# Two transformer blocks on one core: the first MoE's experts by falling count, four of them with 32 slots, and its fallback branch in mid-stage

## The chip, the cores and the metric

The kernel runs on one core of a Trainium2 chip. Its time is the device time of one execution in microseconds. The profile is of one execution. PE is TensorE's matmuls, PEld its weight loads, DVE is VectorE, ACT ScalarE, POOL GpSimd, SP SyncE, whose only work here is to issue DMAs.

## What is computed

256 tokens of width 1024 pass through two blocks of two layers each. The change lies in `grouped_moe` of the first block, which runs in both of its layers. Every token chooses one of four groups of experts and two of the four experts in it, so there are 512 choices over 16 experts of hidden width 512:

```python
scores = sigmoid(xt @ router_w)
sel = scores + router_b
group_score = top_k(sel.reshape(-1, 4, 4), 2)[0].sum(-1)      # best group per token
idx = top_k(where(in_best_group, sel, -inf), 2)               # two experts per token
combine = scores at idx, divided by their sum
for e in range(16):
    h = silu(xt @ w_gate[e]) * (xt @ w_up[e])
    out = out + combine[:, e:e + 1] * (h @ w_down[e])
x = layer_norm(ALPHA * x + out)
```

The second block begins with a mixer (`even`) that adds a table of relative position biases to its attention scores. All numbers are fp32.

## The kernel before

**Stages.** The stages run one after the other: mixer A, the first MoE of layer 0 (`moe1`, 141 to 387 us of the span, then its layer norm), mixer B, the first MoE of layer 1 (515 to 757 us, then its layer norm), mixer `even`, a dense FFN, mixer `odd`, and a second MoE with 8 wider experts (`moe2`).

**Loads.** All weights come as chunks of 128 x 2048 fp32 (1 MiB) in one fixed list, the `Stream` (L53). SP issues their DMAs in this order into a ring of 18 places: 12 of the pool `raw` and 6 of the pool `hl`. A DMA can be issued when its place is free, that is when the matmuls that read the chunk 18 earlier are done, and when the DMA that had the same one of 8 completion semaphores before it has landed. An expert of the first MoE has six chunks: gate and up, two each (0 to 3), and down (4 and 5). `pipe1` (L1981) lists them expert by expert: four of expert e, then the two of e - 1.

**One stage of `moe1`** (L924). `route1` gives for each token and expert a weight `cb` and a position `pm` among the expert's tokens, and `cnt`, the count of each expert. Before the loop one fallback test is prepared from the largest count. The loop then runs over the experts 0 to 15 in this order. For every fourth expert, `gather` builds one-hot matrices `S` (DVE) for four experts with 64 slots each, 256 columns, and multiplies the tokens with them, in two fp32r parts (`xth`, `xtl`): 32 matmuls `gps`, whose results are copied to `xe` by ACT and DVE. Per expert:

- `gate_up`: `slot_rows` turns the expert's columns of `pm` and `cb` with four transposes (`slps`) and makes the selection `sT` and the scale `gs` on DVE; then `pair` (L299) multiplies 64 slots with gate and then with up: the two column halves of 256 run side by side, one into partitions 0 to 63 of the output and one into 64 to 127. ACT takes Silu and DVE multiplies (`h`).
- `down` of the expert before it (`yps`), then `slot_out`: ACT scales and rounds to fp32r (`sy`), DVE makes the remainder.
- `hidden`: two transposes of `h` (`tr`), copied by ACT.
- `scatter` of the expert before it: eight fp32r matmuls with 64 rows add its slots to the four accumulators `ya` in PSUM, which hold all 256 tokens.

Of layer 1's expert 0 the first half is computed densely ahead of the stage (`part`). A fp32 matmul has two records in the trace, an fp32r one has one.

**The branch.** After the loop `rest1` (L1063) reads the largest count into a register of PE, DVE, ACT and SP, and if it is over 64 all experts are computed densely for the tokens over the limit. It isn't taken here. Its body has thousands of PE instructions, which PE jumps over. At that place SP waits for all outstanding DMAs. Then `ln_banks` (L501) does the layer norm, DVE statistics first, under 24 matmuls `warm` that keep PE busy, then `lnT` (transposes of the normalised pieces) and the first matmuls of the next stage (`begin`).

**The bias table.** In layer 1 `rel_bias` (L1087) loads a table and a one-hot matrix ahead of expert 1, and ahead of experts 6 to 9 does one matmul each (`bps`), a copy (`tb`) and a DMA to DRAM (`bscr`), which `even` reads back in skewed order (`bias`).

**The order of instructions.** The framework orders each engine's instructions by a model of costs, except where an order is written out (`order`, `manual_schedule`); it moves instructions ahead within a stretch without branches. A branch ends such a stretch on the engines that take part.

The second MoE has already what the change brings to the first: experts by falling count, loads whose address is read from a register (`index2`), and small experts with 32 slots, `quad` (L306) with four matmuls side by side.

Of the kernel before, what the change touches and what calls it, by code (L numbers as in the profile page):

```python
# [41 lines left out]
C_N = 687  # L42

# [90 lines left out]
class Banks:  # L134
# [5 lines left out]
    def tile(self, shape, dt, name, tag=None):  # L140
        if self.pool is not None and tag not in self.tags:
            return self.pool.tile(shape, dt, name=name, tag=tag)
        self.n += 1
        return self.k.p_ps.tile(shape, dt, name=name, tag=f"b{self.banks[self.n % len(self.banks)]}")

# [83 lines left out]
class Kern:  # L229
# [271 lines left out]
    def ln_banks(self, pre, src, gb, pp, begin=None, add=None):  # L501
# [25 lines left out]
        self.warm(WARM)  # L527
# [348 lines left out]

    def turned_hidden(self, h, hh, hl, g, u, pg, tag, after=None):
# [45 lines left out]
    def moe1(self, layer, stream, x, xt, fill, began, begin):  # L923
# [5 lines left out]
        with ExitStack() as st:  # L929
# [17 lines left out]
            bigi = self.most(pool, cnt)  # L947
# [4 lines left out]
            with ExitStack() as st2:  # L952
# [5 lines left out]
                def gather(es):  # L958
                    n = 4
                    S = w2.tile([128, 2, 4, CAP1], F32R, name="S", tag="S", bufs=1)  # L960
                    for t in range(2):
                        nc.vector.tensor_tensor(S[:, t, :n], self.iota[:, None, :CAP1].to_broadcast([128, n, CAP1]),
                                                pm[:, t, es[0]:es[0] + n, None].to_broadcast([128, n, CAP1]), op=OP.is_equal)
                    xs = w2.tile([128, 8, 4, CAP1], F32, name="xe", tag="xe", bufs=1)
                    for i, e in enumerate(es):
                        xe[e] = xs[:, :, i]
                    for k in range(8):
                        ps = pp.tile([128, 4, CAP1], F32, name="gps", tag="mm")
# [7 lines left out]

                def gate_up(e):
                    if e % 4 == 0:
                        gather(range(e, e + 4))
                    slots[e] = self.slot_rows(w2, pp, pm, cb, e, self.c[:, C_CIDX:C_CIDX + 1])  # L980
                    x64 = xe.pop(e)
                    ps = pg.tile([128, 2, 256], F32, name="gu", tag="gu")
# [11 lines left out]
                def hidden(e, h):  # L994
                    ps = pp.tile([128, 2, 2, CAP1], F32, name="tr", tag="mm")
# [9 lines left out]
                def down(e):  # L1005
                    ps = pp.tile([128, 512], F32, name="yps", tag="mm")
                    fs = (1,) if part(e) else (0, 1)
                    for f in fs:
                        w = stream.get(1024, ahead=1 if e == E1 - 1 and f else None)
                        self.pair(ps, [(hs[e][:, k, f], w[k][0][:, 0:512], w[k][0][:, 512:]) for k in range(2)], f == fs[0], f == 1)  # L1010
# [3 lines left out]
                def scatter(e):  # L1014
                    for t in range(2):
                        for c in range(2):
                            if e == 0:
                                self.mm(ya[t][c], self.ident, pre[:, t, half(c, 512)], True, False)
                        for i in range(2):
                            for c in range(2):  # L1020
                                r = half(c, 64)
                                self.mm(ya[t][c], slots[e][0][r, half(t)], ys[e][i][r, :], False, e == E1 - 1 and i == 1)
                    del slots[e], ys[e]

                for e in range(E1 + 1):
                    if layer == 1 and e in (1, 6, 7, 8, 9):
                        self.rel_bias(w2, max(e - 5, 0), pp)
                    h = gate_up(e) if e < E1 else None
                    if e == E1:
                        begin.allow()  # L1030
                        stream.prepare(3)
                    if e > 0:
                        down(e - 1)
                    if e < E1:
                        hidden(e, h)
                    if e == E1:
                        begin.load()
                        gb = self.load_ln(2 * layer + 1)
                    if e > 0:
                        scatter(e - 1)  # L1040
            self.rest1(layer, bank, x, cb, pm, bigi, part)
            xt = self.ln_banks(pre, bank, gb, Banks(self, (0, 1)), begin)
# [15 lines left out]
    def left(self, pool, pm, cb, cap, n):  # L1058

        w = pool.tile([128, 2, n], F32, name="left")  # L1060
        self.nc.vector.tensor_scalar(w, pm, float(cap), None, op0=OP.is_ge)
        self.nc.vector.tensor_tensor(w, w, cb, op=OP.mult)
        return w  # L1063

    def rest1(self, layer, bank, x, cb, pm, bigi, part):

        nc, tc = self.nc, self.tc
        rv = nc.values_load(bigi[0:1, 0:1], engines=BRANCH, min_val=0, max_val=T)
        with tc.If(rv > CAP1):
            with ExitStack() as st:  # L1070
                p1 = st.enter_context(tc.tile_pool(name=f"rest{layer}", bufs=1))
                pg, py = Banks(self, (0, 1)), Banks(self, (2, 3))
                room = st.enter_context(tc.tile_pool(name=f"rr{layer}", bufs=2))
                wt = self.left(p1, pm, cb, CAP1, E1)
                xt = self.turned(x, pg, "rg", True)
                for e in range(E1):
                    fs = (1,) if part(e) else (0, 1)
                    w = Stream(self, self.chunks1(layer, e, [j for f in fs for j in (2 * f, 2 * f + 1, 4 + f)]), ahead=0, room=room)
                    self.dense1(w, xt, wt, e, fs, bank, p1, pg, py)

    def chunks1(self, layer, e, which, whole=True):

        i = (layer * E1 + e) * 6
        return [(self.a["w_moe1"][i + j], 2, whole) for j in which]


    def rel_bias(self, pool, h, pp):  # L1087


        nc, a = self.nc, self.a  # L1090
        if h == 0:
            self.bscr = self.p_d.tile([4, 23, 512], F32, name="bscr")
            self.relt = pool.tile([32, 4], F32, name="relt", bufs=1)
            nc.sync.dma_start(self.relt, a["relt"])
            self.oh = pool.tile([32, 512], F32, name="oh", bufs=1)
            nc.sync.dma_start(self.oh, a["oh"])
            return
        h -= 1
        rb = pool.tile([32, 128], F32, name="relb", bufs=1)
        nc.vector.tensor_copy(rb, self.relt[:, h:h + 1].to_broadcast([32, 128]))  # L1100
        ps = pp.tile([128, 512], F32, name="bps", tag="mm")
        nc.tensor.matmul(ps, rb, self.oh, start=True, stop=True)
        tb = pool.tile([128, 512], F32, name="tb", bufs=1)
        nc.scalar.activation(tb, ps, AF.Copy)
        nc.scalar.dma_start(self.bscr[h], tb[0:23])
# [427 lines left out]
    def route2(self, pool, w2, pp, ps):  # L1533
# [28 lines left out]
        self.ranked = (idxi, {})  # L1562
# [33 lines left out]
    def index2(self, r):  # L1596

        idx, regs = self.ranked
        if r not in regs:
            regs[r] = self.nc.values_load(idx[0:1, r:r + 1], engines=[ET.SP], min_val=1, max_val=E2 - 1)  # L1600
# [32 lines left out]
    def chunks2(self, jobs):  # L1633
# [3 lines left out]
        def chunk(r, j):  # L1637
# [4 lines left out]
            return (lambda: w[bass.ds(self.index2(r), 1), j].rearrange("o p f -> (o p) f")), 2, r >= HEAVY  # L1642
# [9 lines left out]
    def moe2(self, stream, x, xt, began, ln, out):  # L1652
# [5 lines left out]
        with ExitStack() as st:  # L1658
# [76 lines left out]
            def down(r, s, h):  # L1735
# [21 lines left out]
                def collect(q, y):  # L1757
                    if "small" not in ys:
                        ys["small"] = w2.tile([128, 1024], F32, name="yq", bufs=1)
# [207 lines left out]
    def run(self, out):  # L1967
# [13 lines left out]
        def pipe1(layer, part):  # L1981

            c = []
            for e in range(E1 + 1):
                if e < E1:
                    c += self.chunks1(layer, e, (2, 3) if part and e == 0 else (0, 2, 1, 3))
# [238 lines left out]
```

## Time and profile before

| | us |
|---|---|
| three runs | 1957.87, 1952.04, 1956.91 |
| median | 1956.91 |
| the profiled execution | 1956.97 |
| its span, first to last instruction | 1955.2 |
| PE busy in the span | 1822.1 (93%) |
| DVE, ACT, POOL busy | 892.0, 735.9, 297.8 |
| DMA, mean over the span | 301 GB/s |
| mean granted clock of PE | 0.976 of 2.4 GHz |

Busy time counts overlapping records once, and the ends of matmuls are modelled: consecutive groups overlap by 0.07 to 0.2 us in the rows, so the time of a group is best read from its start to the next one's start. A DMA share of 1.0 means that all 16 DMA engines are busy. Idle time stands in square brackets with what ended it.

### The profile page before, as it was taken

The numbers are of one execution on the slowest core, as the hardware profiler recorded it, in microseconds if no ns is written. First come the engines' busy times: TensorE is split into PE (matmuls) and PEld (weight loads), VectorE is DVE, ScalarE is ACT, GpSimd is POOL, SyncE is SP. The second block draws the span as 40 slices with busy tenths as digits, with TensorE's granted clock in tenths as the row PEclk, the third lists the DMA queues.
The fourth block names the chain that finished last, engine by engine and source line by source line (L and its number), as shares of the span: only waits on it lengthen the run. The fifth ranks groups of instructions, "written<-read, shape, count | busy, mean of one in ns | idle before, by whom it ended". The sixth has DMA issues, their size and how long they took to land. (4 is left out here: it accounts for less than half of the span.)

```text
span 1955.2 us, 36295 instructions
## 1 busy us (share of the span) xinstructions
PE 1822.1 (93%) x15228; PEld 1424.6 (73%) x15228; DVE 892.0 (46%) x1631; ACT 735.9 (38%) x1205; POOL 297.8 (15%) x129
## 2 busy tenths in 40 slices
PE   9999999899999998998999988899998889999896
PEld 8885555488655555897999867787777778987753
DVE  5661121267411113467101476655556568866412
ACT  5531111054211111652444364344445456655311
POOL 0310000002000000523888323200000000000000
PEclk9999999999999999999999999899999999999898
DMA  9659999855598894744553240489999999899995
GB/s 381 249 193 409 409 419 419 326 198 191 192 414 347 340 419 168 288 169 159 181 187 130 88 177 23 172 323 391 388 416 418 418 419 415 343 391 419 419 415 231
DMA packets 86031, 589.29 MB, mean 301 GB/s; under 512 B 9782, under 2 KB 11510, under 8 KB 16340
## 3 DMA queue, kind: packets, MB, share of 16 engines
q1 hardware_dynamic: 83042, 580.67, 74.6%
q10 hardware_dynamic: 2802, 6.06, 0.9%
q8 instruction: 126, 2.06, 0.4%
q14 instruction: 61, 0.50, 0.1%
HBM read 585.45 MB, written 1.24 MB: 300 GB/s over the span
## 5 line engine op out<-in xcount | busy, mean ns | idle before, releaser
L103 ACT ACTIVATE whl<-raw 128x1024 fp32r<-128x1024 f32 x426 | 433.1, 1054 | 220.4 <-issue 98.4
L105 DVE TENSOR_TENSOR whl<-raw,whl 128x1024 fp32r<-128x1024 f32 x315 | 375.2, 1228 | 128.1 <-ACT whl L103 125.8
L105 POOL TENSOR_TENSOR whl<-raw,whl 128x1024 fp32r<-128x1024 f32 x111 | 274.3, 2489 | 898.5 <-ACT whl L103 845.2
L287 PE MATMUL sgu<-whl,xe 128*128 128x256 f32 x2064 | 261.2, 287 | 27.2 <-DVE sh L1705 21.5
L287 PEld LDWEIGHTS sgu<-whl,xe 128*128 128x128 f32 x2064 | 252.7, 193 | 36.4 <-DVE sh L1705 26.5
L287 PE MATMUL gu<-raw,xe 128*64 128x256 f32 x1408 | 172.4, 382 | 0.0
L287 PEld LDWEIGHTS gu<-raw,xe 128*64 128x64 f32 x1408 | 102.0, 137 | 53.7 <-issue 5.3
L287 PE MATMUL fgu<-xh,whl 128*128 128x256 f32 x640 | 116.7, 283 | 0.0
L287 PE MATMUL zps<-xh,whl 128*128 128x256 f32 x576 | 111.5, 291 | 2.6 <-ACT xh L276 1.8
L990 ACT ACTIVATE h<-gu 128x256 f32<-128x256 f32 x31 | 11.9, 383 | 253.6 <-PE gu L287 253.6
L1948 POOL TENSOR_TENSOR pre<-pre,lngb 128x512 f32<-128x512 f32 x2 | 2.5, 1259 | 672.5 <-ACT pre L1947 672.5
L287 PEld LDWEIGHTS fgu<-xh,whl 128*128 128x128 f32 x640 | 100.3, 192 | 0.4
L991 DVE TENSOR_TENSOR h<-h,gu 128x256 f32<-128x256 f32 x31 | 13.1, 422 | 184.8 <-ACT h L990 184.8
L287 PEld LDWEIGHTS zps<-xh,whl 128*128 128x128 f32 x576 | 92.8, 195 | 3.9 <-ACT xh L276 2.0
L287 PE MATMUL fgu<-xl,whl 128*128 128x256 f32 x320 | 90.4, 283 | 0.0
L287 PE MATMUL yps<-raw,hT 128*64 128x512 f32 x352 | 89.5, 595 | 0.0
L287 PE MATMUL zps<-xl,whl 128*128 128x256 f32 x288 | 82.7, 287 | 0.8 <-DVE xl L277 0.8
L287 PE MATMUL sy<-whl,shh 128*128 128x512 f32 x264 | 82.7, 394 | 0.0
L1688 ACT ACTIVATE sh<-sgu 128x256 f32<-128x256 f32 x43 | 16.5, 383 | 159.1 <-PE sgu L287 159.1
L317 DVE SCALAR_TENSOR_TENSOR sy<-yps,gs,sy 128x512 fp32r<-128x512 f32 x32 | 24.0, 751 | 113.7 <-ACT sy L316 113.7
L287 PE MATMUL gu<-whl,xe 128*64 128x256 f32 x608 | 75.5, 383 | 0.0
L1380 DVE TENSOR_TENSOR fh<-fh,fgu 128x512 f32<-128x512 f32 x10 | 6.9, 689 | 139.7 <-PE fgu L287 139.7
(490 smaller groups left out, 3180.5 us busy)
## 6 DMA issues: line engine op xcount, KB each, us to landing
raw<-in_w_moe_dram SPq DMA_DIRECT2D x399, 1024.0 KB, 11.9
whl<-in_w_moe_dram SPq DMA_DIRECT2D x57, 1024.0 KB, 11.0
raw<-in_w_dense_dram SPq DMA_DIRECT2D x53, 1024.0 KB, 7.0
raw<-in_w_ffn_dram SPq DMA_DIRECT2D x33, 1024.0 KB, 6.0
lngb<-in_lnp_dram ACTq DMA_DIRECT2D x8, 512.0 KB, 4.5
lngb<-in_lnp_dram SPq DMA_DIRECT2D x8, 512.0 KB, 5.0
xraw<-in_xT_dram SPq DMA_DIRECT2D x4, 256.0 KB
raw<-in_w_dense_dram SPq DMA_DIRECT2D x2, 512.0 KB, 4.7
```

Of the source, the lines that this page charges most:

```text
L103: nc.scalar.activation(hi, r, AF.Copy)
L105: on.tensor_tensor(lo, r, hi, op=OP.subtract)
L287: self.nc.tensor.matmul(out, lhsT, rhs, start=start, stop=stop, skip_group_check=True)
L317: self.nc.vector.scalar_tensor_tensor(yl, ps, gate, yh, op0=OP.mult, op1=OP.subtract)
L990: nc.scalar.activation(h, ps[:, 0, :], AF.Silu)
L991: nc.vector.tensor_tensor(h, h, ps[:, 1, :], op=OP.mult)
L1380: nc.vector.tensor_tensor(h, h, g[1], op=OP.mult)
L1688: nc.scalar.activation(h, ps[:, 0, :], AF.Silu)
L1948: nc.gpsimd.tensor_tensor(v, v, gb[0][:, half(c, 512)], op=OP.mult)
```

## The change

- `ranks1`, new, sorts experts 3 to 15 by falling count after the first gather (DVE), gives the sorted `pms` and `cbs`, an index per rank and a limit per expert: 64 slots, and 32 for the four of rank 9 to 12.
- The loop runs in `ORDER`: experts 0 to 2 as they are, then ranks, the four light ones (12 to 15) in places 4, 5, 7 and 8. Their loads are register-addressed.
- A gather serves 3, 6 (two with 64 slots, four with 32), 4 and 3 experts.
- A light expert uses `quad`, has its output collected in `yq`, and the four share one `slot_rows` and one `scatter` with 128 slots.
- The register load for the branch stands after place 11 and the branch after place 13, with the largest excess over the limits; the fallback's tiles lie in those of the stage.
- `rel_bias` moves to the end of layer 0, after its loop, with all four heads and one DMA; its loads are on ACT's queue behind the branch. `ln_banks` of layer 0 has 6 `warm` instead of 24.

```diff
+FIXED = 3
+LIGHT = range(E1 - 4, E1)
+ORDER = [0, 1, 2, 3, 12, 13, 4, 14, 15, 5, 6, 7, 8, 9, 10, 11]
+GROUPS = [[0, 1, 2], [3, 4, 12, 13, 14, 15], [5, 6, 7, 8], [9, 10, 11]]
...
+    def ranks1(self, layer, pool, tmp, pm, cb, cnt):
+        n = E1 - FIXED
+        sq, sh = [128, n, n], [128, 2, n, n]
+        nc.vector.scalar_tensor_tensor(key, cnt[:, FIXED:], 16.0, self.iota[:, 0:n], op0=OP.mult, op1=OP.subtract)
+        nc.vector.tensor_tensor(gt, key[:, None, :].to_broadcast(sq), key[:, :, None].to_broadcast(sq), op=OP.is_gt)
+        nc.vector.tensor_reduce(rank, gt, axis=AX.X, op=OP.add)
...
+        self.ranked = (idxi, {}, layer * E1 + FIXED, layer * E1 + E1 - 1)
+        for name, src in (("pms", pm), ("cbs", cb)):
+            nc.vector.tensor_tensor(v, perm[:, None].to_broadcast(sh), src[:, :, None, FIXED:].to_broadcast(sh), op=OP.mult)
+            nc.vector.tensor_reduce(o[:, :, FIXED:], v, axis=AX.X, op=OP.add)
...
                 def gate_up(e):
-                    if e % 4 == 0:
-                        gather(range(e, e + 4))
-                    slots[e] = self.slot_rows(w2, pp, pm, cb, e, self.c[:, C_CIDX:C_CIDX + 1])
+                    if e in LIGHT:
+                        ps = pg.tile([128, 2, 128], F32, name="lgu", tag="gu")
+                        for i in range(2):
+                            w = enumerate(zip(stream.get(256), stream.get(256)))
+                            self.quad(ps[:, i, :], [(x64[:, k], *(v[0][:, half(j)] for v in (g, u) for j in range(2))) for k, (g, u) in w])
+                        nc.scalar.activation(v[up], ps[lo], AF.Silu)
+                        nc.vector.tensor_tensor(v[up], v[up], ps[up], op=OP.mult)
+                        return h
+                    rows(e)
...
                 def down(e):
+                    if e in LIGHT:
+                        ps = pp.tile([128, 256], F32, name="lps", tag="mm")
+                        for i in range(2):
+                            w = stream.get(1024)
+                            self.quad(ps, [(hs[e][:, i, half(k, 32)], *(w[k][0][:, half(j, 256)] for j in range(4))) for k in range(2)], i == 0, i == 1)
+                        for j in range(4):
+                            nc.scalar.activation(ys["light"][half(e - LIGHT[0], 32), half(j, 256)], ps[half(j, 32)], AF.Copy)
+                        return
...
                 def scatter(e):
+                    if e in LIGHT:
+                        if e != LIGHT[-1]:
+                            return
+                        rows(LIGHT)
+                        y = [self.slot_out([v[:, c] for v in room], ys["light"][:, half(c, 512)], slots[LIGHT][1]) for c in range(2)]
+                        for i in range(2):
+                            for t in range(2):
+                                for c in range(2):
+                                    self.mm(ya[t][c], slots[LIGHT][0][:, half(t)], y[c][i], False, False)
+                        return
...
-                for e in range(E1 + 1):
-                    if layer == 1 and e in (1, 6, 7, 8, 9):
-                        self.rel_bias(w2, max(e - 5, 0), pp)
+                for i, e in enumerate([*ORDER, None]):
+                    if i == 0:
+                        gather(groups[e], pm)
+                        pms, cbs, cap, bigi = self.ranks1(layer, pool, w2, pm, cb, cnt)
+                    elif e in groups:
+                        gather(groups[e], pms)
...
+                    if i == E1 - 5:
+                        rv = nc.values_load(bigi[0:1, 0:1], engines=BRANCH, min_val=0, max_val=T)
+                    if i == E1 - 3:
+                        self.rest1(layer, w2, bank, x, cb, pm, cap, rv, part)
+                        if layer == 0:
+                            rel = self.rel_load(w2)
+                if layer == 0:
+                    self.rel_bias(*rel, w2, pg)
-            self.rest1(layer, bank, x, cb, pm, bigi, part)
-            xt = self.ln_banks(pre, bank, gb, Banks(self, (0, 1)), begin)
+            xt = self.ln_banks(pre, bank, gb, Banks(self, (0, 1)), begin, warm=WARM if layer else 6)
...
+    def rel_load(self, pool):
+        nc.scalar.dma_start(relt, a["relt"])
+        nc.scalar.dma_start(oh, a["oh"])
+        nc.vector.tensor_copy(rb, relt[:, :, None].to_broadcast([32, 4, 128]))
+        return rb, oh
+    def rel_bias(self, rb, oh, pool, pp):
+        for h in range(4):
+            ps = pp.tile([128, 512], F32, name="bps")
+            nc.tensor.matmul(ps, rb[:, h], oh, start=True, stop=True)
+            nc.scalar.activation(tb[0:23, h], ps[0:23], AF.Copy)
+        nc.scalar.dma_start(self.bscr.rearrange("h p f -> p h f"), tb[0:23])
...
+        return [(lambda j=j: w[bass.ds(self.index(e - FIXED), 1), j].rearrange("o p f -> (o p) f"), 2, whole) for j in which]
```

## Rows read from the trace of the kernel before

**Rows 1.** Windows of both stages: from:to, length, busy per engine, clock, DMA share, GB/s.

```profile
141.20:386.73 245.53, 238.73 (x1667) 131.73 (x1665) 42.59 (x109) 29.53 (x66) 0.00 (x0) 1.00 0.97 395
...
515.30:757.35 242.05, 236.06 (x1614) 128.84 (x1612) 45.16 (x112) 31.40 (x70) 0.00 (x0) 1.00 0.88 354
```

**Rows 2.** Windows inside the first stage and near its end.

```profile
220.00:235.00 15.00, 15.00 (x112) 8.28 (x110) 2.73 (x7) 1.34 (x3) 0.00 (x0) 1.00 1.01 420
...
359.00:361.00 2.00, 2.00 (x20) 1.19 (x18) 0.00 (x0) 0.25 (x1) 0.00 (x0) 1.00 0.04 16
```

**Rows 3.** Timeline of SP's issues: start, us to the last issue, what, count.

```profile
332.52 12.19 SPq L76 DMA_DIRECT2D raw<-in_w_moe_dram  x6
...
503.42 13.64 SPq L76 DMA_DIRECT2D whl<-in_w_moe_dram  x5
```

**Rows 4.** Timeline of PE around ordinary experts.

```profile
278.91 0.43 PE L844 MATMUL slps<-consts,pm 128*128 128x128 f32 x2
...
291.84 0.43 PE L844 MATMUL slps<-consts,pm 128*128 128x128 f32 x2
...
385.22 1.51 PE L287 MATMUL ya<-sy,sT 64*128 64x512 f32 x8 [0.79 <-ACT sy L316]
```

**Rows 5.** Timelines of PE and DVE in the second MoE, experts with 32 slots.

```profile
1495.18 1.96 PE L287 MATMUL sgu<-raw,xq 128*32 128x128 f32 x64
1496.95 1.05 PE L287 MATMUL sy<-raw,lhT 128*32 128x256 f32 x16
...
1887.21 0.33 PE L844 MATMUL slps<-consts,slsp 128*128 128x128 f32 x1
...
1889.42 3.67 PE L287 MATMUL sgu<-raw,xl 128*64 128x256 f32 x32
...
1891.27 1.41 DVE L317 SCALAR_TENSOR_TENSOR sy<-yq,gs,sy 128x512 fp32r<-128x512 f32 x2 [0.79 <-ACT sy L316]
...
1900.59 2.12 PE L287 MATMUL fy<-sy,sT 128*128 128x512 f32 x8
```

**Rows 6.** A group of PE instructions by form; the first stage's window, `gps` alone.

```profile
L287 PE MATMUL begin<-raw,xf 128*128 128x256 f32 x192 | 44.5, 385 | 0.0
...
141.20:386.73 245.53, 20.67 (x128) 16.50 (x128) 6.80 (x16) 6.14 (x16) 1.00 0.97 395
```

**Rows 7.** The branch's line on SP and PE (ns; first and last start); PE's stops.

```profile
L1069 SPq EVENT_SEMAPHORE  x16: 17/17/17, 360.4 to 745.6; - x16
L1069 SPq COMPARE_BRANCH  x2: 45/48/50, 348.7 to 728.7; - x2
...
L1069 PEldq COMPARE_BRANCH  x2: 3549/4891/6233, 386.7 to 757.2; - x2
...
386.73:392.97 6.24, 0.00 (x1) 0.00 (x0) 6.03 (x20) 0.00 (x0) 0.00 (x0) 0.69 0.78 315
757.35:760.84 3.49, 0.01 (x2) 0.00 (x0) 1.10 (x2) 0.00 (x0) 0.00 (x0) 1.00 0.04 9
```

**Rows 8.** Timelines of DVE, PE and ACT at the ends of stages.

```profile
391.00 1.67 DVE L515 SCALAR_TENSOR_TENSOR pre<-pre,lnrs,lngb 128x256 f32<-128x256 f32 x4
...
393.11 4.12 PE L287 MATMUL warm<-bfconst 128*128 128x256 bf16 x24 [6.38 <-PEq L1069]
397.06 0.38 PE L535 MATMUL lnT<-consts,pre 128*128 128x128 f32 x2
...
767.50 0.38 ACT L536 ACTIVATE xf<-lnT 128x256 f32<-128x256 f32 x1 [11.72 <-DVE lnv L405]
...
1107.18 2.79 PE L287 MATMUL warm<-bfconst 128*128 128x256 bf16 x24
```

**Rows 9.** Bias matmuls (PE), the count (DVE), and SP's waits in layer 1's stage.

```profile
511.46 0.16 DVE L811 COPY cnt<-posps 128x16 f32<-128x16 f32 x1
...
614.97 1.12 PE L1102 MATMUL bps<-oh,relb 32*128 32x512 f32 x2
...
SPq L76 <- DMA bscr<-tb: 57.6, 4, 18.4
```

More of the change, by code (lines that the diff above doesn't have):

```diff
@@ L499, in out_proj, with ln_banks @@
         return pre, xt
-    def ln_banks(self, pre, src, gb, pp, begin=None, add=None):
+    def ln_banks(self, pre, src, gb, pp, begin=None, add=None, warm=WARM):
         nc = self.nc
@@ L526, in ln_banks @@
         xf = self.p_raw.tile([128, 8, 256], F32, name="xf", tag="raw")
-        self.warm(WARM)
+        self.warm(warm)
         for t in range(2):
@@ L994, in hidden @@
                 def hidden(e, h):
+                    if e in LIGHT:
+                        ps = pp.tile([128, 2, 64], F32, name="tr", tag="mm")
+                        for j in range(2):
+                            nc.tensor.transpose(ps[:, j], h[up, half(j)], self.ident[up, up])
+                        hs[e] = w2.tile([128, 2, 64], F32, name="lhT", tag="hT", bufs=1)
+                        nc.scalar.activation(hs[e], ps, AF.Copy)
+                        return
                     ps = pp.tile([128, 2, 2, CAP1], F32, name="tr", tag="mm")
@@ L1067, in rest1 @@
         nc, tc = self.nc, self.tc
[L1068 to L1087, printed above, removed]
-        nc, a = self.nc, self.a
[L1091 to L1105, printed above, removed]
+        with tc.If(rv > 0):
+            p1 = Rooms(w2, {"left": "left", "rhh": "yq", "rh": "S"})
+            pg, py = Banks(self, (0, 1)), Banks(self, (2, 3))
+            room = InTurn(self.p_c, ("lng", "lnb"))
+            wt = self.left(p1, pm, cb, cap, E1)
+            xt = self.turned(x, pg, "rg", True)
+            for e in range(E1):
+                fs = (1,) if part(e) else (0, 1)
+                w = Stream(self, self.chunks1(layer, e, [j for f in fs for j in (2 * f, 2 * f + 1, 4 + f)]), ahead=0, room=room)
+                self.dense1(w, xt, wt, e, fs, bank, p1, pg, py)
@@ new lines, in chunks1 @@
+    def chunks1(self, layer, e, which, whole=True, ranked=False):
+        w = self.a["w_moe1"]
+        if not ranked or e < FIXED:
+            return [(w[layer * E1 + e, j], 2, whole) for j in which]
+        return [(lambda j=j: w[bass.ds(self.index(e - FIXED), 1), j].rearrange("o p f -> (o p) f"), 2, whole) for j in which]
+    def rel_load(self, pool):
+        nc, a = self.nc, self.a
+        relt = pool.tile([32, 4], F32, name="relt", bufs=1)
+        nc.scalar.dma_start(relt, a["relt"])
+        oh = pool.tile([32, 512], F32, name="oh", tag="S", bufs=1)
+        nc.scalar.dma_start(oh, a["oh"])
+        rb = pool.tile([32, 4, 128], F32, name="relb", tag="yq", bufs=1)
+        nc.vector.tensor_copy(rb, relt[:, :, None].to_broadcast([32, 4, 128]))
+        return rb, oh
@@ L1983, in pipe1 @@
             c = []
-            for e in range(E1 + 1):
-                if e < E1:
-                    c += self.chunks1(layer, e, (2, 3) if part and e == 0 else (0, 2, 1, 3))
-                if e > 0:
-                    c += self.chunks1(layer, e - 1, (5,) if part and e == 1 else (4, 5))
+            for e, last in zip([*ORDER, None], [None, *ORDER]):
+                if e is not None:
+                    c += self.chunks1(layer, e, (2, 3) if part and e == 0 else (0, 1, 2, 3) if e in LIGHT else (0, 2, 1, 3), ranked=True)
+                if last is not None:
+                    c += self.chunks1(layer, last, (5,) if part and last == 0 else (4, 5), ranked=True)
             return c
@@ L2202, in expert @@
         return [g[0], u[0], g[1], u[1], _chunk(d[:256], 0, D), _chunk(d[256:], 0, D)]
-    a["w_moe1"] = np.stack([c for l in range(2) for e in range(E1) for c in expert(l, e)])
+    a["w_moe1"] = np.stack([np.stack(expert(l, e)) for l in range(2) for e in range(E1)])
     a["w_ffn"] = np.stack(_gate_up(f["ffn_w_gate_2"][0], f["ffn_w_up_2"][0]) + _downs(f["ffn_w_down_2"][0]))
```

119 lines of the change are left out of this document (88 added, 31 removed).

## The prediction

> **What bounds the kernel now.** I read the stretches of the two expert stages first, then TensorE's instructions in order of time, then the load queue, and last the branch. In both stages TensorE is busy for 97 and 98% of the stretch at a granted clock of 1.00, which is 2.4 GHz [rows 1]. The weight loads are close behind: in the middle of the first stage the DMA share is 1.01 at 420 GB/s [rows 2], so a chunk of 1 MiB takes 2.5 us and the six of an expert 15.0 us. An ordinary expert costs TensorE 12.93 us from one `slps` to the next [rows 4], and each group of four a gather of 32 `gps` matmuls. So two streams of nearly the same pace run beside each other, and what matters is how far loads run ahead. The last load of the first stage was issued before 345 us [rows 3], nothing moved at 359 to 361 us [rows 2], and the last matmuls that read a chunk ended at 384.4 us, where the wait before the last `ya` begins [rows 4]: loads were done some 25 us before their last use. The path to the end of a stage is therefore TensorE's, and it can be cut by some 20 to 25 us before loads set the pace. In the second stage loads had slack (share 0.88, [rows 1]).
>
> **Light experts, per layer.** Four experts leave the ordinary path: 4 x 12.93 = 51.7 us. In their place each does gate and up with 32 columns: second-MoE rows of the same form show 1.96 us for 64 records of `sgu` and 1.05 us for 16 of `sy` per slice of 256 [rows 5], two slices per expert: 6.0 us, and its transposes some 0.4 (as now, inside the 12.93): 4 x 6.4 = 25.6 less the overlaps of some 0.1 us at each change of group, 23.5. Once per layer come four transposes with a copy ahead of each (1887.21 to 1889.42: 2.2 us) and eight scatter matmuls with 128 slots (2.1 us) [rows 5]. Sum 27.8, so -23.9. The scatter also waits for selection, scale and split, which in the second MoE were hidden behind other matmuls; with nothing to hide them it costs 3.2 (from the last transpose, 1889.4, to the end of the second split, 1892.7 [rows 5]); I take 1.6. Some experts of the later half wait 0.79 us for `sy` before `ya` [rows 4], early ones don't. If all twelve do, +5, if none, -6; I take +2, because the branch cuts the stretch over which instructions are ordered together.
>
> **Gathers.** The groups become 3, 6, 4 and 3 experts: 192, 256, 256 and 192 columns. Now four gathers of 256 columns take 20.7 us, 5.2 each and 0.16 per matmul [rows 6]. No row has fp32r under 256 columns. From below it costs three quarters (-1.3 us per gather). From above it loses its single pass and costs three quarters of what plain fp32 with 256 columns does: 192 records, two per matmul, in 44.5 us [rows 6], 0.46 us each, so 0.35 against 0.16, 32 x 0.19 = +6 per gather. Four such gathers: -5 to +24. I take the nearest row, the same operands at 256 columns: 0.
>
> **Branch in the middle, per layer.** Now TensorE stands still behind the branch: 6.24 us in the first layer, DMA share 0.78, and 3.49 us in the second, share 0.04 [rows 7].  In the middle of the stage the share is 1.01, so by the line through these two points the stop is 7.1 us. Behind it TensorE starts at a lower clock: 24 `warm` matmuls took 4.12 us after the stop and 2.79 where nothing stopped [rows 8], so I add 1.5. Sum 8.6; bounds 3.5, and 17 if it stands as long as SP does at its branches (11.7 and 16.9 us from its compare to its first event after it [rows 7]). Queued behind the branch on PE are the next expert's `gu` matmuls, which ACT, DVE and the loads' slots wait for. SP's stop also makes a hole in the loads: the DMA share of 0.04 at 359 to 361 us is that hole [rows 2]. It lies now after the last expert's chunks and will lie 13 chunks earlier; about 4 us of lead, no time while lead is left.
>
> The Trainium skill (Runtime: NRT & Kernel Launch, Instruction fetch mechanics) says that a taken branch whose target isn't among the pages held forces a fetch by DMA before execution goes on. By that rule the fetch stands in line with loads, which the two stops at shares 0.04 and 0.78 bear out; the sum by the rule alone would reach for the upper end, 8 us more per layer, and by the row of an idle DMA 4 us less.
>
> **End of the stages.** In layer 0 `warm` began after the stop and `lnT` at 397.06 us, while DVE had its first normalised piece at 391.5 [rows 8]. After the change PE does four bias matmuls of the form `bps` there (1.12 us for one [rows 9], some 4.2 in all; their copies are on an idle ACT) and 6 instead of 24 `warm`: `lnT` at about 392.0, -5.0. The path behind it is PE's own. In layer 1 ACT issued the DMAs of the next block until 767.5, after PE's release at 760.8, and only then copied `lnT` [rows 8]; without the stop of 3.5 us all of it is that much earlier: -3.5.
>
> **Bias table.** In layer 1 four `bps` go from TensorE's path: -4.2. Four waits of SP for `bscr` (57.6 us in total [rows 9]) go too; they cost no time now, but loads. In layer 0 the two small loads on ACT's queue and the copy of `relt` come after the branch; if DVE waits for the landing, up to 5 us in front of the next `h`; the later `gu` (7 us) hides it, 0.
>
> **Ranks and loads.** DVE adds some 25 small operations per layer at its idle start; the second stage's five loads at 503.42 to 517 us [rows 3] are partly of ranked experts and must now wait for the ranks, which can't come before `cnt` at 511.5 [rows 9] plus seven operations and SP's register load, about 515. Five loads are 12.5 us of lead. With the light experts in the first half TensorE gains 24 us on the loads up to the ninth expert, about what the lead is at the end, so it may then wait for loads: 0 to 4 us in layer 0, 0 to 10 in layer 1; I take 1 and 4. Register-addressed loads themselves exist in the second MoE and cost SP some 0.2 us against 2.5 per chunk: 0.
>
> **Sum.** Layer 0: -23.9 + 1.6 + 2 + 8.6 + 1 - 5.0 = -15.7. Layer 1: -23.9 + 1.6 + 2 + 8.6 + 4 - 4.2 - 3.5 = -15.4. Together -31.1. The profiled execution took 1956.97 us (span 1955.2 and 1.8 around it), the median of three is 1956.91, so no correction: 1926 us. Its own range, from the bounds of branch (-5 to +8 per layer) and bubbles, mostly independent, 1914 to 1940.
>
> **Rivals.**
> *Narrow gathers are slow.* All terms as above and +24 for four gathers of 192 columns at the plain fp32 pace: 1950 us. For it: moe2's gathers of 128 columns use plain fp32. Against it: the 256-column rows are not bound by columns alone (weight loads of 128 columns stand beside them).
> *Loads set the pace (slower).* If the lead is used up early, the light experts give nothing, since every chunk is still loaded. Then the hole of SP at the branch (4 us) and the wait for the ranks (5) cost in full in both layers and so does the chain at the branch (8.6), against -5.0, -3.5 and -4.2: 2 x 17.6 - 12.7 = +22, 1979 us. It decides from the point where the landing is less than some 2 us ahead of its use before the ninth expert; the 25 us at the end of the first stage speak against it, the share of 1.01 for it.
> *The fallback runs.* The change lowers four limits to 32. If an expert among the last four had more than 32 tokens, all 16 are computed densely, 96 more chunks x 2.5 = 240 us in that layer. Counted from the reference's inputs, the lightest four of experts 3 to 15 have 27, 24, 19, 15 tokens in layer 0 and 24, 22, 22, 16 in layer 1, and no expert over 53: not taken.
> *More than forecast.* Branch at 3.5 without a clock loss, gathers at three quarters, no waits for loads or bubbles: -31 - 10 - 5 - 5 - 4 = -55, 1902 us.
>
> **Chances.** Forecast 0.52, narrow gathers slow 0.26, loads set the pace 0.10, more than forecast 0.11, fallback 0.01. A measurement of this kernel tells 0.3% (5.9 us) from no change. All of the forecast and of the larger gain is faster, of the slow gathers two thirds (1950 lies at the edge): faster 0.82; same 0.11 (a third of the slow gathers, and a little of the load case); slower 0.07. Eight in ten: 1905 to 1953.
>
> **What would show it.** Right: the light experts' `gu` take 3.9 us and the group from its first `gu` to the next ordinary expert some 7 us less each; one PE stop in mid-stage of about 7 us and none before `warm`; `lnT` about 5 us after the last `ya` of layer 0; share about 1.0 through 600 to 665 us. Wrong: `gps` of 192 columns with 0.3 us of pitch or more; PE waiting for `raw` behind the light experts; a mid-stage stop over 12 us; SP standing at the ranks for over 10 us; SP or DVE waiting for `relt` in layer 0.

## The result, and the profile after

The changed kernel takes 1933.04 us (median of four runs, 1931.05 to 1937.26) against 1954.47 (four runs): ratio 0.9892, 95% interval 0.9874 to 0.9911, or -21.4 us. Forecast were 1926 and a range of 1905 to 1953. The profiled execution took 1931.05 us, span 1929.3, which is 25.9 below the span of before. Of these, 4.6 lie ahead of the change, in code that both kernels share. One line of the windows each, the first 20 us of before and of after (columns as in [rows 1]):

```profile
0.00:20.00 20.00, 15.62 (x84) 13.19 (x85) 10.03 (x14) 10.20 (x15) 0.19 (x4) 0.83 0.87 331
```
```profile
0.00:20.00 20.00, 16.87 (x118) 14.64 (x119) 10.33 (x15) 11.69 (x16) 0.19 (x4) 1.00 0.90 340
```

The execution of before that was profiled began at a granted clock of 0.83, the one of after at 1.00. The later kernels, alike there, reach the matmuls `posps` ahead of the first stage at 135.0 to 138.2 us (before 140.5, after 135.9). Without that start, -21.3 is left, close to the -21.4 of the medians.

The two stages of the changed kernel, which answer to [rows 1], and what PE waited for in each:

```profile
139.60:373.90 234.30, 214.13 (x1935) 122.26 (x1934) 39.86 (x106) 35.87 (x84) 0.00 (x0) 0.99 0.97 396
503.90:732.40 228.50, 205.66 (x1880) 120.34 (x1880) 41.94 (x116) 31.77 (x78) 0.00 (x0) 0.96 0.94 387
```
```profile
PE ya L314 <- ACT sy L343: 6.6, 8, 1.9
PE slps L871 <- PEq L1191: 6.5, 1, 6.5
PE tr L1080 <- DVE h L1061: 2.0, 2, 1.0
PE slps L871 <- ACT yq L1104: 1.7, 1, 1.7
PE gps L314 <- ACT yq L1104: 1.6, 1, 1.6
...
PE ya L314 <- ACT sy L343: 8.2, 10, 1.9
PE slps L871 <- PEq L1191: 6.5, 1, 6.5
PE gps L314 <- DVE xe L1043: 2.0, 1, 2.0
```

(Columns: who waited for what, us in total, times, longest. PEq and ACTq are the sequencers of PE and ACT, here at the branch.) Counted from the first `gps` to the last `ya`, the first stage went from 242.5 to 234.3 us and the second from 237.7 to 228.5. PE, busy for 97% before, now stands still for 20 us of the first and 23 us of the second. Most of that is 6.5 at the branch, 7.1 in the chains of the light experts, 4.7 and 6.3 ahead of the ordinary experts' `ya` (6.3 and 5.5 before), and 2.0 at the first gather of layer 1. It waits nowhere for a chunk.

The light experts in layer 0, PE's timeline (start, us, instruction, idle before):

```profile
228.15 3.70 PE L314 MATMUL lgu<-raw,xe 128*32 128x128 f32 x128
232.82 0.34 PE L1080 MATMUL tr<-consts,h 64*128 64x64 f32 x2 [0.98 <-DVE h L1061]
...
243.66 0.33 PE L1080 MATMUL tr<-consts,h 64*128 64x64 f32 x2 [0.98 <-DVE h L1061]
243.92 1.93 PE L314 MATMUL lps<-whl,lhT 128*32 128x256 f32 x32
247.50 0.50 PE L314 MATMUL gps<-S,xth 128*128 128x256 f32 x2 [1.65 <-ACT yq L1104]
...
264.71 0.33 PE L871 MATMUL slps<-consts,slsp 128*128 128x128 f32 x1 [1.66 <-ACT yq L1104]
...
269.03 2.28 PE L314 MATMUL ya<-sy,sT 128*128 128x512 f32 x8 [1.86 <-ACT sy L343]
```

3.70 and 1.93 us are what [rows 5] foretold (3.9 and 2.1); the five idle times add up to 7.1. The mid-stage stop in layer 0, and the end of that stage:

```profile
328.72 1.52 PE L314 MATMUL ya<-sy,sT 64*128 64x512 f32 x8 [0.42 <-ACT sy L343]
...
336.78 0.66 PE L871 MATMUL slps<-consts,pms 128*128 128x128 f32 x2 [6.53 <-PEq L1191]
...
373.81 0.83 PE L314 MATMUL warm<-bfconst 128*128 128x256 bf16 x6
378.51 1.91 PE L562 MATMUL lnT<-consts,pre 128*128 128x128 f32 x6 [3.87 <-DVE pre L542]
...
381.49 8.00 PE L314 MATMUL begin<-raw,xf 128*128 128x256 f32 x30
```

`lnT` begins 4.6 us after the last `ya`, when DVE has its first piece; in [rows 8] it was 10.3.

### The profile page after: what moved, and what is told of

It reads as the page before. It is cut to its first block, busy times and chain, and to the rows that moved or that the text cites. A ratio compares the mean times of both kernels' runs of the same rounds, so it can differ in the third digit from the quotient of the medians.

```text
span 1929.3 us, 37804 instructions
## 1 busy us (share of the span) xinstructions
PE 1772.0 (92%) x15778; PEld 1410.5 (73%) x15778; DVE 893.7 (46%) x1655; ACT 744.7 (39%) x1233; POOL 297.3 (15%) x129
## 5 line engine op out<-in xcount | busy, mean ns | idle before, releaser
L314 PE MATMUL gu<-raw,xe 128*64 128x256 f32 x960 | 115.2, 390 | 0.0
L314 PEld LDWEIGHTS gu<-raw,xe 128*64 128x64 f32 x960 | 70.8, 141 | 38.4 <-issue 6.5
L1815 DVE TENSOR_TENSOR sh<-sh,sgu 128x256 f32<-128x256 f32 x43 | 18.1, 421 | 113.3 <-ACT sh L1814 113.0
L314 PE MATMUL yps<-raw,hT 128*64 128x512 f32 x288 | 69.3, 597 | 0.0
L314 PE MATMUL gu<-whl,xe 128*64 128x256 f32 x544 | 66.1, 383 | 0.0
```

The lines of the kernel that those rows point to most:

```text
L314: self.nc.tensor.matmul(out, lhsT, rhs, start=start, stop=stop, skip_group_check=True)
L1815: nc.vector.tensor_tensor(h, h, ps[:, 1, :], op=OP.mult)
```

## Experiments

Each kernel is the changed one with the edit shown. Differences to it are the difference of the two ratios to before times 1955 us; with the intervals of both, they are known to some 5 us. All kernels ran on a chip beside the kernel before.

**all64**: no light experts.

```diff
-FIXED = 3
-LIGHT = range(E1 - 4, E1)
+FIXED = 4
+LIGHT = range(E1, E1)
+ORDER = [*range(E1)]
+GROUPS = [[0, 1, 2, 3], [4, 5, 6, 7], [8, 9, 10, 11], [12, 13, 14, 15]]
```

> The changed kernel without light experts: all sixteen keep 64 slots and run in the order 0 to 15 after sorting from the fourth on; four gathers of 256 columns; branch in mid-stage, bias table and 6 warm as in the changed kernel. My theory: the light experts are the one real gain in the stages, 51.7 us of ordinary work against 23.8 (records), 3.2 (scatter), 7.1 (waits of PE for h, yq and sy), and 1.2 less for the narrow gathers, so 18.8 per layer. Without them 37 us slower than the changed kernel, about 1970, which is some 0.8% slower than before. Rival (loads set the pace of the stages, so that PE's saving is partly hidden): under 20 us slower than the changed kernel, below 1953, and PE waiting for raw in the changed kernel's stages instead.

1961.49 us, ratio 1.003 (1.0019 to 1.0041): 27 slower than the changed kernel, and slower than before. So without the light experts the other parts together cost 6 us; which of them cost and which gain, this run does not tell. Of the 37 expected, 10 are missing in the medians, but not in the profiles: from `posps` to the last `ya` the two stages take 17.6 and 14.4 us longer. In layer 0 the stop of all64 was 2.8 shorter, and in layer 1 the changed kernel lost 3.7 at its gather (below); with these it is 20.4 and 18.1 per layer, against 18.8. The profiled run of all64 was the slowest of eight and that of the changed kernel the fastest of four, so part of this is chance. The rival is out: PE waits for no chunk in either kernel.

**end_branch, no_branch, warm24**: the branch behind the stage again; no branch; 24 `warm` in layer 0.

```diff
 # end_branch, in the loop and behind it
-                        self.rest1(layer, w2, bank, x, cb, pm, cap, rv, part)
+            self.rest1(layer, None, bank, x, cb, pm, cap, rv, part)   # tiles in pools of its own, as before
 # no_branch
-                        rv = nc.values_load(...)
-                        self.rest1(layer, w2, bank, x, cb, pm, cap, rv, part)
 # warm24
-            xt = self.ln_banks(..., warm=WARM if layer else 6)
+            xt = self.ln_banks(..., warm=WARM)
```

> The changed kernel with its fallback branch back behind the stage (register loads stay in mid-stage). My theory: the mid-stage stop is a pure loss on PE, 6.5 and the slow clock behind it 1.4 in layer 0, 6.5 and 2.8 in layer 1; at the end the stop lies beside the layer norm's statistics, which hold lnT for 4.6 us anyway, so it costs only what it is longer plus the warm matmuls behind it: about +2 in layer 0 (6 warm) and +3 in layer 1 (24 warm). Together -12 against the changed kernel: about 1921, ratio to before 0.983. Rival (the move was neutral: what the mid-stage stop costs, the end gives back, as the terms 8.6 against -5.0 and -3.5 of the forecast nearly have it): -5 or less, 1928 to 1935.

> The changed kernel without its fallback branch and register load (leaves out the fallback, which these inputs never take). My theory: both stops and the slow clock behind them go and nothing else takes their place, since PE nowhere waits for a load in the changed kernel's stages: -7.9 in layer 0 and -9.3 in layer 1, about 1916, ratio 0.980. Rival (loads catch up: 17 us less of PE leave the chunks late): -8 or less, 1925, with PE waiting for raw in the last four experts.

> The changed kernel with 24 instead of 6 warm matmuls in layer 0's norm. My theory: after 6 of them PE is idle for 3.9 us, the granted clock falls and the first 30 begin records take 8.0 us instead of some 6.6; 24 take 2.8 us, which lies inside the 4.6 us of the statistics, so nothing is added and begin gets its 1.4 us back: -1.4, 1931.6; lnT at the same distance of 4.6 us from the last ya. Rival (the few warm matmuls of the change are what brings lnT forward): lnT 1 to 3 us later and the time +1 to +3.

end_branch: 1922.42, ratio 0.9832 (0.9815 to 0.9848), -12. no_branch: 1914.49, 0.9799 (0.9785 to 0.9813), -18. warm24: 1930.54, 0.9876 (0.986 to 0.9892), -3 and inside the error, but its trace has the 28 `begin` in 6.21 us, 0.22 each against 0.27 above, with `lnT` at the same 4.6 us. end_branch and no_branch came out as the theory had it, in time: the change made the branch dearer by moving it. At the end the stop lies beside statistics that hold `lnT` for 4.6 us anyway (with the stop there `lnT` came 8.3 and 11.3 us after the last `ya`); in mid-stage nothing lies beside it. By layers end_branch's profile, 8.7 us shorter, fits less well. Its stages are 4.0 and 9.2 us shorter (7.9 and 9.3 expected), and the stretches from the last `ya` to the second half of `begin` are 2.2 and 3.9 longer; in layer 0 the clock fell behind the light experts' waits instead (last section). The time of warm24 can't tell its theory from the rival; its trace bears the theory out. In the 18 us of no_branch, loads did not become late: PE waits for no chunk.

**tiny_body**: what the stop is made of.

```diff
-            for e in range(E1):
+            for e in range(0):        # in rest1
```

> The changed kernel with a fallback body of 16 transposes on PE instead of thousands of instructions (leaves out the dense experts of the fallback, which these inputs never take); the test, its register load and its place in mid-stage stay. My theory: the stop is the way over the body, instructions that must be fetched before PE can go on, so with a short body PE stops under 1 us in both layers and the clock does not fall: -7.4 and -8.8, about 1917, ratio 0.981. Rival (the stop belongs to the taken branch itself, or to the busy DMA engines: any jump under load costs it): 6 us in both layers as now, no difference, 1933.

1916.63, ratio 0.9801 (0.9785 to 0.9817), -18: nearly all that no_branch gained. The branch's line on PE, in the changed kernel and with the short body (ns: shortest, median, longest of two):

```profile
L1191 PEldq COMPARE_BRANCH  x2: 6177/6282/6386, 330.2 to 689.2; - x2
```
```profile
L1191 PEldq COMPARE_BRANCH  x2: 228/282/337, 323.5 to 676.8; - x2
```

The taken branch took 0.3 us where it jumps a little way and 6 where it jumps over the fallback. The Trainium skill (Runtime: NRT & Kernel Launch, Instruction fetch mechanics) says that a taken branch to instructions not held must fetch them by DMA before going on; the traces agree. The DMA queues in the changed kernel's stop (330.2 to 336.4 us: packets, MB, share) hold instruction packets, in the short one's (323.4 to 323.8) none:

```profile
q1 hardware_dynamic: 342, 2.54, 99.3%
q8 instruction: 1, 0.02, 1.0%
q14 instruction: 2, 0.02, 0.6%
```
```profile
q1 hardware_dynamic: 23, 0.16, 99.2%
```

By itself this is no proof, since such packets also pass where nothing stops (two in 310.0 to 316.2 us). But in the second stop of the kernel before (757.2 to 760.7 us) they are all that moved:

```profile
q8 instruction: 1, 0.02, 2.1%
q14 instruction: 2, 0.02, 1.8%
```

The edit empties the bodies of the other engines too: ACT's first event comes 0.1 us after its branch, where it took 6.3 and 2.5 in the changed kernel. So the 18 us need not be PE's stop alone; hint, below, parts the two.

**chain, act_gather**: the light experts' waits, and layer 1's first gather.

```diff
 # chain
+                            if j % 2: nc.vector.tensor_copy(dst, ps[half(j, 32)])     # yq: every other copy on DVE
+                        with tc.issue_after(self.last.ins):                           # tr of a light h behind the last down matmul
+                    if i > 1 and ORDER[i - 2] == LIGHT[-1]:
+                        scatter(LIGHT[-1], True)                                      # one expert later, sT and gs in places of their own
 # act_gather
-                        if k % 2:
+                        if k % 2 and not on_act:                                      # on_act: first gather of layer 1
```

> The changed kernel with the light experts' waits loosened: yq's copies shared by ACT and DVE, the common scatter one expert later (under the gate and up of the next), and the transposes of a light h behind the down matmuls of the expert before. My theory: the waits of 0.98 (twice), 1.65, 1.66 and 1.86 us of PE in each stage are chains with nothing beside them; two halve and three go: about -5.4 per layer, 1922, ratio 0.984. Rival (they only move: the next ordinary expert's ya and h then wait in their place): -2 per layer or less, 1929 or more.

> The changed kernel with all eight copies of the first gather on ACT in layer 1. My theory: the DVE operations of the ranking lie ahead of the copies there, PE waits 2.03 us for one of them and then runs 20 gps at a lower clock (4.58 us instead of 2.9): -4 in layer 1, 1929, PE without a wait in that gather. Rival (ACT's copies are then what gps wait for, or the clock was low for another reason): 0 to +2, 1933 to 1935.

chain: 1918.82, ratio 0.9811 (0.9797 to 0.9825), -16, more than the 11 expected; in its profile the stop was 3.4 us in both layers instead of 6.3, which is 5.8 of it and not what the edit aimed at: its branch met DMA engines that were partly idle (last section). PE's waits in layer 0 became

```profile
PE slps L871 <- PEq L1199: 3.6, 1, 3.6
PE ya L314 <- ACT sy L343: 3.3, 6, 0.8
PE slps L871 <- ACT hT L1094: 0.9, 1, 0.9
PE gps L314 <- ACT lhT L1084: 0.5, 1, 0.5
```

so of the 7.1 us 1.4 are left (the last two lines), and they did not move to the ordinary experts. act_gather: 1932.28, 0.9877 (0.9857 to 0.9898), -3, which can't be told from nothing. Its trace has no wait in that gather, but 1.0 us of waits for chunks in layer 1; in both layers the clock then fell at the light experts' waits (their eight `ya` took 3.78 us instead of 2.28).

**bias1**: the bias table back in layer 1.

```diff
+                    if layer == 1 and i in (1, 6, 7, 8, 9):
+                        self.rel_bias(w2, max(i - 5, 0), pp)      # and rel_bias as before
```

> The changed kernel with the bias table built in layer 1 as before (five pieces ahead of experts 1 and 6 to 9 of the order, loads on SP's queue, four DMAs), none of it in layer 0. My theory: a swap of equal work: layer 0 wins some 3.4 us (the four matmuls of 1.1 us there partly fill waits for sy), layer 1 loses 4.2 and SP waits for bscr; no difference that can be told, 1930 to 1936. Rival (the move is worth its own gain, since layer 1's SP waits of 57.6 us delay loads of a stage that now has no slack): 4 us or more slower, 1937, with PE waiting for raw in layer 1.

1942.14, ratio 0.9928 (0.9913 to 0.9942), +7. My expectation of no difference failed; the rival is nearer. Layer 1's stage, from `posps` on, is 10.2 us longer in its profile, and PE waits there for a chunk as it did not before:

```profile
PE lps L314 <- DMA whl<-in_w_moe_dram: 1.9, 1, 1.9
```

The matmuls themselves are 4.5 of it. Part of the rest is the clock: as an estimate, from PE's busy time in windows of 1 us times what the granted clock there lacks of 1.00, bias1 lost 10.3 us in this stage and the changed kernel 7.1. In layer 0, where bias1 has four matmuls fewer, its stage is not 3.4 us shorter, as expected, but 1.3 longer, with 6.3 us lost to the clock against 1.5, most of it ahead of the branch, where both kernels do the same work. So the +7 can't be put down to the bias table alone.

**hint**: the fetch begun early.

```diff
+                    if i == E1 - 3:                                # behind gate_up, ahead of down
+                        with tc.issue_after(self.last.ins):
+                            tc.mark_branch_hint_location(f"rest{layer}", "LikelyTaken", engines=[ET.PE])
-        with tc.If(rv > 0):
+        with tc.If(rv > 0, label=f"rest{layer}"):
```

> The changed kernel with one instruction more on PE per layer: a branch prefetch hint between the gate-and-up and the down matmuls ahead of the branch, some 6 us before it. Body and place of the branch are unchanged. My theory: the stop is the fetch of the instructions behind the body, which begins only at the branch (3.4 to 3.9 us where the DMA engines are idle in its first 3 us, 6.0 to 6.5 where they are busy); begun 6 us ahead it is over in time: stop under 1 us, no clock loss, time as with the short body, 1917, ratio 0.980. Rival (the hint comes to nothing, or its fetch waits behind the weights and ends no earlier than the branch needs it): stop of 3 us or more, 1925 to 1933.

1926.42, ratio 0.9853 (0.9835 to 0.9871), -8: the mechanism holds, the sum does not. The time lies in the rival's range, but not for the rival's reason: PE's branch takes under half a microsecond with the body unchanged, at a DMA share of 1.02 in the 3 us from its start in layer 0:

```profile
L1194 ACTq COMPARE_BRANCH  x2: 50/52/54, 330.8 to 685.9; - x2
...
L1194 PEldq COMPARE_BRANCH  x2: 439/464/488, 331.9 to 686.9; - x2
...
L1194 ACTq EVENT_SEMAPHORE  x2: 17/17/17, 336.2 to 688.6; - x2
```

but ACT also jumps over its body, and its first event behind the branch came 5.4 us later in layer 0 and 2.7 in layer 1. PE then waits for ACT, 1.6 us in layer 1 and in layer 0

```profile
336.27 0.69 PE L871 MATMUL slps<-consts,pms 128*128 128x128 f32 x2 [4.30 <-ACTq L1194]
```

**best1, best2, best3**: the parts together. best1 is end_branch, chain and act_gather with 10 `warm` in layer 1; best2 is hint, chain, act_gather and warm24; best3 adds to best2

```diff
+                        for on, last in ((ET.PE, self.last), (ET.Activation, self.silu)):   # hint on both
-        nc.scalar.dma_start(gup, a["gup"])
+        nc.gpsimd.dma_start(gup, a["gup"])                 # strict, and bias of heads 0 and 1, likewise
```

> Branch behind the stage, loosened light experts and the first gather's copies on ACT together, with 10 instead of 24 warm matmuls in layer 1's norm. My theory: they lie on different stretches of PE's path and add: -11 (branch), -11, -4, and -2 for the fewer warm matmuls behind the stop: about 1905, ratio 0.975. Rival (the loads become the bound once PE has gained 25 us: PE waits for raw in the last experts, and the gains don't add): 1912 or more.

> The changed kernel with the prefetch hint, the loosened light experts, the first gather's copies on ACT in layer 1, and 24 warm matmuls in layer 0's norm. My theory: -16 (hint), -11 (light experts, without the shorter stop that its run had by chance), -2, -2: 1902, ratio 0.974, less some 3 us of waits for raw as they showed in layer 1 with the branch behind the stage: 1905. Rival (loads now set the pace of both stages): PE waits over 8 us for raw and whl, 1910 or more.

> The kernel before this one (prefetch hint on PE, loosened light experts, first gather's copies on ACT in layer 1, 24 warm matmuls in both norms) with two things more: the prefetch hint also on ACT, and the six DMAs of the next mixer's first tables on POOL's queue instead of ACT's at the end of layer 1. My theory: with PE's own fetch hidden, PE waited 1.3 us in each layer for ACT, whose fetch is now hidden too: -2; and ACT's issues, 10 us in a row, stood ahead of its copies of lnT, which made PE wait 5.6 us: -5. Together 1906, ratio 0.975, still some 3.5 us of waits for raw and whl in layer 1. Rival (what waits passes on: the copies come earlier, but begin then waits for its chunk or for the second half of the norm): 1911 to 1913.

best1: 1912.81, ratio 0.9785 (0.977 to 0.98); best2: 1913.0, 0.978 (0.9764 to 0.9796); best3: 1908.49, 0.9762 (0.9748 to 0.9775), the lowest, with the fallback whole. The first two missed their 1905 and lie in their rivals' ranges. In best1 PE reaches the loads in layer 1, 3.6 us, and its stop behind the stage was the long one:

```profile
PE warm L314 <- PEq L1199: 5.9, 1, 5.9
...
PE lgu L314 <- DMA raw<-in_w_moe_dram: 1.7, 1, 1.7
PE lps L314 <- DMA whl<-in_w_moe_dram: 1.3, 1, 1.3
...
PE lps L314 <- DMA raw<-in_w_moe_dram: 0.6, 1, 0.6
```

In best2 ten microseconds of DMA issues on ACT, at the end of layer 1, stood ahead of its copy of `lnT`:

```profile
715.15 5.00 ACTq L1271 DMA_DIRECT2D strict<-in_strict_dram  x1
...
720.20 4.63 ACTq L1404 DMA_DIRECT2D bias<-bscr  x4
...
725.31 1.11 PE L562 MATMUL lnT<-consts,pre 128*128 128x128 f32 x4 [5.64 <-ACT xf L563]
```

Issued by POOL in best3 they left PE 0.47 us of that wait; the stretch from the last `ya` to the second half of `begin` became 7.7 us shorter, but the next one, up to the FFN's first matmul, 2.8 longer. The hint on ACT did not do its part: PE still waited 1.4 and 1.5 us for ACT, whose first event came 2.6 us after its branch (2.5 and 2.4 in best2, without that hint). The rivals for best1 and best2, that loads set the pace, fit only layer 1, by 3.6 and 3.5 us, where best2's named over 8.

## Why the prediction was right, step by step

The direction and the range held, and the forecast of 1926 was 7 us low. Of the change itself -31.1 were forecast and -21.4 measured, 10 too much; 2.5 of these do not show in the 7, because the kernel before took 1954.47 beside the changed one and not 1956.91. The terms did worse than the sum. The light experts' chains cost 11 us more than I took and layer 0's end 5.5 more, and more than half of that is made up by waits that I priced and that did not come: 5 for loads and 4.8 ahead of ordinary `ya`. That part of the agreement is luck. Per layer, in us, from the profiles:

| step | forecast | layer 0 | layer 1 |
|---|---|---|---|
| light experts, their own work | -23.9 | -24.6 | -24.6 |
| PE's waits for their chains | +1.6 | +7.1 | +7.1 |
| waits ahead of ordinary `ya` | +2 | -1.6 | +0.8 |
| gathers | 0 | -1.2 | -1.2, +3.7 |
| branch and clock behind it | +8.6 | +7.9 | +9.3 |
| waits for loads | +1, +4 | 0 | 0 |
| bias table | in the end's -5.0; -4.2 | +4.2 | -4.2 |
| end of stage | -5.0, -3.5 | -5.7, +2.0 | -3.2 |

Layer 0 gives -11.9, layer 1 -12.3; between them 0.9 us are lost ahead of the second stage and 2.2 behind it, together -21.1.

- **Light experts: right.** 51.7 [rows 4] against four times 5.96 (3.70, 1.93 and 0.33 above) and 3.3 for the common scatter.
- **The chain: mis-sized.** I priced one wait, for the common scatter, at 1.6 with 3.2 as its upper end. It is 3.5 (1.66 and 1.86), and three more were not in the sum: `tr` for `h`, twice, and `gps` for the four `yq` copies that hold a PSUM bank. The rows of the second MoE [rows 5] could not show them, since other matmuls lie beside them there. A light expert halves PE's work but not the chain from PE over ACT and DVE back to PE. chain shows that these waits were avoidable. The 7.1 is also a mild case: where the clock falls behind these waits, they cost some 4 us more per layer (last section), and the changed kernel's profile was spared that.
- **Gathers: right to take no loss.** 32 `gps` of 192 columns take 4.56 us against 5.2 [rows 6], so the rival of slow narrow gathers is out. What I had not seen is the queue: in layer 1 the ranking's operations stand on DVE ahead of the gather's copies, PE waits 2.03 us, the clock falls, and 20 `gps` take 4.58 instead of 2.98.
- **Branch: right in size, and now in mechanism.** 6.5 and 1.4 to 2.8 of slow matmuls against 7.1 and 1.5. But I priced the move as a shift: the stop at the end was already half paid by the layer norm's statistics. end_branch would have given 12 us.
- **Loads: not the bound.** SP did stand at the ranks, for 19.6 us in layer 1, where I had named over 10 as a sign of being wrong. It cost PE nothing here: PE waits for no chunk, and behind the ranks the loads ran at a share of 1.01 (600 to 665 us, as forecast). SP also waited 9.7 us for `oh` in layer 0, close to another of the signs, again at no cost to PE. The lead was small: act_gather, bias1 and the three last kernels show PE at the loads in layer 1.
- **End of layer 0: half wrong.** `lnT` came at 4.6 us as forecast, but I let the four bias matmuls lie under the statistics; they run ahead of the last `ya` and cost their 4.2. Six `warm` and 3.9 us of idle then cost 2.0 in `begin`: its first half took 10.2 us, and 8.3 in warm24.
- **Slips in the sum.** The rows of `warm` give 1.3 (4.12 less 2.79) and not 1.5; twelve waits of 0.79 us would be +3 to +4 and not +5; the chances for faster add up to 0.80 and not 0.82. Together they move the forecast by less than half a microsecond.

## What to carry to other kernels

Price a smaller tile by its chain as well as by its matmuls: of the 24.6 us per layer that PE saved here, the round trips over ACT and DVE took 7.1 back where no other tile's matmuls lay beside them. A branch over a long body held PE for 3.4 to 6.5 us and ACT for 2.4 to 6.3, so put it where the engines wait anyway, make the body short, or have the target fetched ahead on every engine that others wait for (the hint did this on PE; on ACT it changed nothing). After each gain look at who is next: here ACT's branch, ACT's DMA issues, then the loads.

## What the runs showed of the hardware

**The stop has two lengths, which go with the DMA load.** DMA share in the first 3 us of the stop (3.5 for before's second), and the length of PE's branch record:

| share | stops | us |
|---|---|---|
| 0.04 to 0.12 | before 1, all64 0, end_branch 0, chain 0, best1 0 | 3.35 to 3.66 |
| 0.41, 0.61 | chain 1, end_branch 1 | 3.49, 3.91 |
| 0.87 to 1.03 | before 0, all64 1, best1 1, both of after, act_gather, warm24, bias1 | 5.84 to 6.45 |

before, all64 and best1 show both lengths in one kernel; no run sets the DMA load by itself. My line through two points happened to hold the two levels. hint fits: begun ahead of the branch, the fetch is hidden though the body stays and the share is 1.02. ACT's way from its branch to its first event behind it has two lengths as well, 2.4 to 2.7 us and 4.3 to 6.3, and 0.1 with the short body.

**One wait of 2 us can be followed by half the clock.** Windows in the changed kernel around layer 1's first gather (the column before the DMA share is the granted clock; 0.50 is 1.2 of 2.4 GHz):

```profile
503.90:505.90 2.00, 1.87 (x13) 1.56 (x12) 1.93 (x10) 0.37 (x2) 0.00 (x0) 1.00 0.00 0
505.90:507.90 2.00, 0.04 (x1) 0.04 (x1) 2.00 (x9) 0.29 (x1) 0.00 (x0) 0.80 0.00 0
507.90:512.40 4.50, 4.50 (x21) 4.50 (x22) 1.22 (x5) 0.66 (x2) 0.00 (x0) 0.50 0.90 322
512.40:520.00 7.60, 7.60 (x59) 4.63 (x59) 3.33 (x12) 0.65 (x2) 0.00 (x0) 0.90 1.01 423
```

It fell so in five of the seven profiles that have this wait (after, no_branch, tiny_body, warm24, chain); in hint and end_branch, after the same wait of 2.03 us, the 20 `gps` took 2.98. (Here the clock had also been lower earlier, 0.69 at 495 to 498 us; in warm24 it had been 1.00 from 480 us on.)

The light experts' waits of 1.66 and 1.86 us did the same in some profiles. Layer 0 behind them, the changed kernel and end_branch:

```profile
266.00:270.00 4.00, 2.13 (x8) 1.08 (x9) 2.13 (x6) 1.34 (x2) 0.00 (x0) 1.00 1.01 420
```
```profile
266.00:270.00 4.00, 2.39 (x7) 0.82 (x5) 1.37 (x5) 0.52 (x1) 0.00 (x0) 0.50 1.01 420
```

In end_branch, act_gather and bias1 it fell in both layers, and the eight `ya` took 3.78 us instead of 2.28; in end_branch this cost some 4.2 us per stage, by the estimate used for bias1. With chain's edit the eight `ya` took 2.4 in every profile.
